# Second layer of a flow block: three buffers for split weights, 56 rows ahead with 14 parked, gathers over all rows, and a moved fold

## The chip, the cores and the metric

The kernel runs on one core of one Trainium2 chip. Its time is the device time of one execution, in microseconds (us). Five engines work beside each other, each on its own in-order queue: PE (matrix products; PEld is its loading of weights), DVE (vector work), ACT (scalar functions, copies, casts), POOL (here the indirect gathers) and SP (which issues most transfers). ACT and POOL issue some transfers too; 16 DMA engines carry all of them.

## The reference

Two layers, each with a mixer (gated unit, state-space scan, linear attention) and an expert part. The change touches the expert part of the second layer, for 256 tokens:

```python
def peer_ffn(h, w_query, sub_keys, expert_u, expert_v):    # blocks of 128 tokens
    q = (xb @ w_query).reshape(128, 8, 2, 128)
    s = einsum('thpd,phkd->thpk', q, keys)                 # 128 keys in each half
    s1, i1 = top_k(s[:, :, 0], 16);  s2, i2 = top_k(s[:, :, 1], 16)
    top_s, pos = top_k(s1[..., :, None] + s2[..., None, :], 16)
    idx = take_along_axis(i1 * 128 + i2, pos)              # 16 of 16384 experts, for each of 8 heads
    gate = softmax(top_s)
    act = gelu(einsum('td,thkd->thk', xb, expert_u[idx]))
    return einsum('thk,thkd->td', gate * act, expert_v[idx])
```

All is float32. Then follow a residual with a gate row and the last norm.

## The kernel before, in words

**Dense rows.** Instead of gathering 128 experts for each token, the kernel goes through all 16384 experts as 128 rows of 128 (NI1 = 128) and weighs what a token did not choose with zero. Row e has two halves. `U(e)` loads 128 vectors of expert_u (512 KB), splits them into a rounded part hi (ACT, L72) and a rest lo (DVE, L73), and PE multiplies both with the tokens (L1376, L1380) into the PSUM tile pu; ACT and DVE sum its two parts and apply GELU (L1398 to L1400). `V(e)` loads 128 vectors of expert_v, splits them the same way, multiplies the activations with the gates of row e (DVE, L1423), splits that product into whl (L1426 to L1429), and PE adds to four PSUM tiles acc (L1445). `stream` loads into `eraw` (five buffers) and has two buffers each for uhi, ulo, vhi and vlo.

**Gathered part.** In the second layer 192 of the 256 tokens go the dense way. For the other 64, `gather_rows` fetches the chosen experts' vectors by indirect DMA on POOL (L1300, 512 KB each): 64 u-items, which DVE multiplies and sums (L1306), and 64 v-items, which DVE adds into gacc (L1313). They share four `grow` buffers.

**Order.** `LEAD` rows of U are computed before the first V. They need only the tokens; the V rows need the gates, which `gates` makes at the same time: DVE writes one-hot matrices (108 operations, L1245 to L1253), PE multiplies them, ACT scales the result into a staging tile gst (two buffers of 16 KB a partition), and ACT's queue writes it to DRAM as gd (2 MB, six times, L1263). The gates of the first 8 rows stay on the chip; those of the others are read back as gt, four rows at a time (L1415). After the lead, V rows run alone until row LEAD - KEEP; from there each V row is paired with a U row. The first 8 activations of the lead stay in a buffer, the next `SPILL` rows are parked in DRAM (`aout` out, L1403; `ain` back, L1408), the rest stay on the chip.

`side()` is called once for each V row and once for each U row behind the lead. It adds `RATE` to an account, and takes the next gather items while the account is positive. The last three V rows go together (TOGETHER = 3). Then the 64 upper and 64 lower partitions of the last dense block are folded and joined to gacc by PE (L1514 to L1522), and the tail scales, adds, norms and stores.

A scheduler sets the final order of each engine's queue, so that the order in the program is a preference; a buffer's next writer waits for its last readers.

Of the kernel before, what the change touches and what calls it, by code (L numbers as in the profile page):

```python
# [10 lines left out]
F32 = mybir.dt.float32  # L11
F32R = mybir.dt.float32r
# [4 lines left out]
OP = mybir.AluOpType  # L17
# [11 lines left out]
PLAN = {"s5": ((4, 1, 0, 0, 0, 0), (4, 0, 0, 0, 0, 0)), "gla": ((1, 1, 1, 1, 0, 1, 1), (2, 2, 1, 1, 0, 1))}  # L29
DEPTH = 2  # L30
NI1 = 128
LEAD = {0: 40, 1: 64}
KEEP = 4
HOLD = {0: 4, 1: 8}
TOGETHER = {0: 4, 1: 3}
SPILL = {0: 22, 1: 32}
AHEAD = 2
ERAW = 5
GPS = 3
OHT = 8  # L40
OHB = 3
OSC = "av"
RATE = {0: 2.4, 1: 1.0}
NEG = -3.0e38


# [4 lines left out]
class Kernel:  # L51
# [1276 lines left out]
    def peer(self, l, dense):  # L1328
        nc, i = self.nc, self.i
        nb = len(dense)  # L1330
        half = self.half[l]
# [5 lines left out]
        with ExitStack() as es:  # L1337
            p = es.enter_context(self.pool(f"peer{l}"))
            acts_a = es.enter_context(self.pool(f"acta{l}"))
            es_b = es.enter_context(ExitStack())  # L1340
            acts_b = es_b.enter_context(self.pool(f"actb{l}"))
            lead, spill = LEAD[l], SPILL[l]
            per, away = 1024 // nt, {}
# [6 lines left out]
            p2 = es.enter_context(self.pool(f"peerv{l}", side="right"))  # L1350
            acc = [[pa.tile([128, 512], F32, name=f"acc{b}{h}", bufs=1) for h in range(2)] for b in range(nb)]
            acts, gt, rows, todo, left, los = {}, {}, {}, [], [], []

            def stream(src, nm):
                raw = p.tile([128, 1024], F32, name="eraw", bufs=ERAW)
                nc.sync.dma_start(raw, src)
                hi = p.tile([128, 1024], F32R, name=nm + "hi", bufs=2)
                lo = p.tile([128, 1024], F32R, name=nm + "lo", bufs=2)
                self.split(hi, lo, raw)
                return hi, lo  # L1360

# [48 lines left out]
            def V(e):  # L1410
# [6 lines left out]
                late = NI1 - 1 - e  # L1417
                hi, lo = stream(i["v"][l, e], "u" if late < TOGETHER[l] and late % 2 else "v")
# [14 lines left out]
                    return  # L1433

                for b in range(nb) if half is None else (1, 0):
                    for hs in ((0,), (1,)) if late == 0 else ((0, 1),):
                        for e_, hi, lo, w in todo:
                            if 128 * b + 128 > nt:

                                ops = [(w[:, 2 * nt - 64:], r) for r in (hi, lo)]  # L1440
                            else:
                                ops = [(w[:, o:o + 128], r) for o, r in ((128 * b, hi), (128 * b, lo), (nt + 128 * b, hi))]
                            for z, (a_, r) in enumerate(ops):
                                for h in hs:
                                    nc.tensor.matmul(acc[b][h], a_, r[:, 512 * h:512 * h + 512],  # L1445
                                                     start=e_ == 0 and z == 0, stop=e_ == NI1 - 1 and z == len(ops) - 1)
                todo.clear()

            def mod_load(l_, n, half):
                raws = []  # L1450
                for q in range(2):
                    raw = p.tile([128, 1024], F32, name="eraw", bufs=ERAW)
                    o = 2048 * half + 1024 * q
                    nc.sync.dma_start(raw, i["w_mod"][l_, n][:, o:o + 1024])
                    raws += [(raw, 0), (raw, 512)]
                return raws

            def pubank(shape, nm):
                t = pu_.tile([128, 512], F32, name="pu", bufs=8 - 2 * nb)
                n = math.prod(shape[1:])  # L1460
                return t[:, :n] if len(shape) == 2 else t[:, :n].rearrange("p (a b) -> p a b", b=shape[2])
            gb = self.gathered[l]
            gg = self.gather_gen(l, gb, es) if gb is not None or half is not None else iter(())
            mg = self.mod_gen(l, range(10, 12), mod_load, pubank, p, False)
            if not last:
# [15 lines left out]
            for e in range(NI1):  # L1481
# [5 lines left out]
                if e + KEEP == NI1:  # L1487
# [3 lines left out]
                    ep = es.enter_context(self.pool(f"peere{l}", side="right"))  # L1491
# [15 lines left out]
            out = {b: (acc[k][0], acc[k][1]) for k, b in enumerate(dense)}  # L1507
            if gb is not None:
                out[gb] = (self.gacc[:, 0:512], self.gacc[:, 512:1024])
            if half is not None:  # L1510

                out[half] = []
                fold = ep.tile([128, 64], F32, name="fold", bufs=1)
                nc.vector.tensor_tensor(fold, self.ident[:, 0:64], self.ident[:, 64:128], op=OP.add)  # L1514
                for h in range(2):
                    t = ep.tile([128, 512], F32, name="ft", bufs=2)
                    nc.scalar.copy(t, acc[nb - 1][h])
                    b = pubank([128, 512], "fold")
                    nc.tensor.matmul(b[0:64], fold, t, start=True, stop=True)
                    nc.tensor.matmul(b[64:128], fold, self.gacc[:, 512 * h:512 * h + 512], start=True, stop=True,  # L1520
                                     tile_position=(0, 64))
                    out[half].append(b)  # L1522
            for k, b in enumerate(sorted(out) if half is None else (3, 2)):
                ty = b // 2
                x = self.xk[b] = self.row([128, 1024], f"xe{b}")
# [2 lines left out]
                for h in range(2):  # L1528
                    hs = slice(512 * h, 512 * h + 512)
                    t = ep.tile([128, 512], F32, name="et", bufs=3)  # L1530
# [14 lines left out]
                else:  # L1545
# [6 lines left out]
                    for h, q in ((0, nc.sync), (1, nc.scalar)):  # L1552
                        hs = slice(512 * h, 512 * h + 512)
# [123 lines left out]
```

## Time and profile before

| | us |
|---|---|
| median of 3 runs (2687.3 to 2694.61) | 2690.12 |
| the profiled execution, its own time | 2692.46 |
| its span, first to last instruction | 2689.2 |
| PE busy (share of the span) | 2525.4 (94%) |
| DVE busy | 2185.1 (81%) |
| ACT busy | 1217.7 (45%) |
| POOL busy | 593.8 (22%) |

The program is a chain of stages, and busy time is a mean over all of them, so the shares in this table don't say what bounds a stage. A busy PE counts pipelined products whose ends are modelled. All that the change touches lies behind 1916 us, where the second layer's first U row is split on DVE.

### The profile page before, as it was taken

To read this page: it belongs to the slowest core of one execution; us is meant where nothing else is said; L and a number is where in the kernel's file an instruction comes from. 1 tells how busy PE (TensorE), PEld (TensorE's weight loads), DVE (VectorE), ACT (ScalarE), POOL (GpSimd) and SP (SyncE) were. 2 spreads that over 40 slices of the span, in tenths; PEclk is the share of its full clock that TensorE was granted. 3 is DMA by queue.
4 is the path that set the end of the run, shared out by engine and by line. 5 is a ranking of instruction groups with operands and counts; after the bars stand their busy time and mean duration, and the time that the engine had idled before them with its cause. 6 is when DMAs were issued, how large, how long until landed. Compare 5 with 4: busy or idle time off the path is not lost.

```text
span 2689.2 us, 42483 instructions
## 1 busy us (share of the span) xinstructions
PE 2525.4 (94%) x15591; PEld 2141.6 (80%) x15591; DVE 2185.1 (81%) x4639; ACT 1217.7 (45%) x2054; POOL 593.8 (22%) x468
## 2 busy tenths in 40 slices
PE   7999999999999999999999999999888977999997
PEld 4776888888778898998899996878877855677786
DVE  8765489999888988998988855837989788999985
ACT  3343343566434333333333333444457644555564
POOL 0001000010004433444443400010001043444500
PEclk8998999999999999999999999989899999999999
DMA  7521432587779899999999956625477899999984
GB/s 271 135 94 41 156 109 93 179 296 280 261 242 371 302 342 333 340 342 331 329 340 335 337 184 176 227 96 192 160 247 264 286 338 331 384 381 381 384 299 141
DMA packets 269200, 694.55 MB, mean 258 GB/s; under 512 B 28608, under 2 KB 120576, under 8 KB 266432
## 3 DMA queue, kind: packets, MB, share of 16 engines
q1 hardware_dynamic: 192960, 430.57, 47.3%
q0 software_dynamic: 55296, 201.35, 20.6%
q10 hardware_dynamic: 20736, 59.92, 6.3%
q8 instruction: 122, 2.00, 0.3%
q14 instruction: 86, 0.70, 0.1%
HBM read 631.84 MB, written 58.56 MB: 257 GB/s over the span
## 4 chain that ended last, share of the span: by engine, by line
PE 41%; issue 12%; DVE 10%; DMA 6%; ACT 4%; ACTq 0%; POOL 0%; SPq 0%; DVEq 0%; POOLq 0%
PE acc L1445 20%; PE pu L78 14%; PE pu L1376 2%; DMA act<-aout 2%; DVE ulo L73 2%; DVE vlo L73 2%; PE pu L1380 1%; ACT uhi L72 1%; DVE grow L1306 1%; DMA ain<-act 1%; ACT vhi L72 1%; PE prT L286 1%; DVE wlo L73 1%; DMA raw<-in_w_in_dram 1%; DVE gacc L1313 1%
## 5 line engine op out<-in xcount | busy, mean ns | idle before, releaser
L1445 PE MATMUL acc<-vhi,whl 128*128 128x512 f32 x2274 | 662.3, 401 | 27.1 <-ACT whl L1426 19.6
L1445 PEld LDWEIGHTS acc<-vhi,whl 128*128 128x128 f32 x2274 | 428.1, 190 | 131.3 <-ACT whl L1426 26.7
L72 ACT CAST vhi<-eraw 128x1024 fp32r<-128x1024 f32 x253 | 265.0, 1048 | 344.1 <-PE acc L1445 308.1
L1445 PE MATMUL acc<-vlo,whl 128*128 128x512 f32 x1264 | 395.4, 404 | 14.5 <-DVE vlo L73 14.0
L78 PE MATMUL pu<-hTb,uhi 128*128 128x384 f32 x2048 | 390.9, 341 | 7.7 <-ACT uhi L72 3.8
L73 DVE TENSOR_TENSOR vlo<-eraw,vhi 128x1024 fp32r<-128x1024 f32 x253 | 309.0, 1223 | 106.9 <-ACT vhi L72 106.3
L1300 POOL DMA_INDIRECT grow<-in_un_dram,gidx x192 | 243.9, 1270 | 603.3 <-DVE grow L1306 198.6
L78 PEld LDWEIGHTS pu<-hTb,uhi 128*128 128x128 f32 x2048 | 362.2, 190 | 17.3 <-ACT actr L1396 4.7
L73 DVE TENSOR_TENSOR ulo<-eraw,uhi 128x1024 fp32r<-128x1024 f32 x259 | 316.7, 1223 | 72.3 <-ACT uhi L72 57.9
L72 ACT CAST uhi<-eraw 128x1024 fp32r<-128x1024 f32 x259 | 272.0, 1051 | 183.5 <-PE pu L78 171.8
L1300 POOL DMA_INDIRECT grow<-in_v_dram,gidx x192 | 271.2, 1412 | 347.1 <-DVE gacc L1313 215.9
L1376 PE MATMUL pu<-hTb,uhi 128*128 128x384 f32 x1024 | 320.7, 369 | 18.0 <-ACT uhi L72 16.0
L1445 PEld LDWEIGHTS acc<-vlo,whl 128*128 128x128 f32 x1264 | 238.9, 191 | 82.8 <-DVE vlo L73 28.7
L1380 PE MATMUL pu<-hTb,ulo 128*128 128x192 f32 x1024 | 250.2, 265 | 25.7 <-DVE ulo L73 24.8
L1313 DVE SCALAR_TENSOR_TENSOR gacc<-grow,gact,gacc 128x1024 f32<-128x1024 f32 x190 | 243.9, 1284 | 1.8 <-DMA grow<-in_v_dram,gidx 1.7
L286 PE MATMUL prT<-hTb,whi 128*128 128x512 f32 (+1 forms) x928 | 240.2, 346 | 3.5 <-ACT whi L72 3.2
L1306 DVE SCALAR_TENSOR_TENSOR grow<-grow,h2n 128x1024 f32<-128x1024 f32 x192 | 234.4, 1221 | 8.8 <-DMA grow<-in_un_dram,gidx 8.8
L1380 PEld LDWEIGHTS pu<-hTb,ulo 128*128 128x128 f32 x1024 | 198.6, 196 | 48.5 <-DVE ulo L73 41.4
L1376 PEld LDWEIGHTS pu<-hTb,uhi 128*128 128x128 f32 x1024 | 195.1, 193 | 27.6 <-ACT uhi L72 22.6
L78 PE MATMUL pu<-hTb,ulo 128*128 128x384 f32 x1024 | 204.0, 337 | 0.5 <-DVE ulo L73 0.5
L73 DVE TENSOR_TENSOR wlo<-raw,whi 128x1024 fp32r<-128x1024 f32 x84 | 102.4, 1220 | 114.0 <-ACT whi L72 111.3
L286 PEld LDWEIGHTS prT<-hTb,whi 128*128 128x128 f32 x928 | 159.8, 190 | 31.3 <-ACT whi L72 3.4
(435 smaller groups left out, 3839.6 us busy)
## 6 DMA issues: line engine op xcount, KB each, us to landing
eraw<-in_ut_dram SPq DMA_DIRECT2D x256, 512.0 KB, 5.6
eraw<-in_v_dram SPq DMA_DIRECT2D x256, 512.0 KB, 6.0
gd<-gst ACTq DMA_DIRECT2D x18, 2048.0 KB, 8.2
mraw<-in_w_mod_dram SPq DMA_DIRECT2D x64, 512.0 KB, 5.1
gt<-gd SPq DMA_DIRECT2D x31, 768.0 KB, 10.2
raw<-in_w_in_dram SPq DMA_DIRECT2D x36, 512.0 KB, 5.3
raw<-in_w_query_dram SPq DMA_DIRECT2D x32, 512.0 KB, 3.9
eraw<-in_w_mod_dram SPq DMA_DIRECT2D x32, 512.0 KB, 6.3
```

What stands on the lines that cost most here:

```text
L72: (hi_eng or nc.scalar.copy)(hi, src)
L73: self.last_lo = (lo_eng or nc.vector).tensor_tensor(lo, src, hi.bitcast(F32), op=OP.subtract)
L78: self.nc.tensor.matmul(out, a, b, start=n == 0, stop=n == len(ops) - 1)
L286: self.nc.tensor.matmul(bs[g][:, pt * n:pt * n + n], a[:, k, gs], b, start=z == 0 and k == 0 and q == 0, stop=z == 1 and k == 3 and q == 2)
L1300: nc.gpsimd.indirect_dma_start(out=r, out_offset=None, in_=src, in_offset=bass.IndirectOffsetOnAxis(ap=idx[:, j:j + 1], axis=0))
L1306: v.scalar_tensor_tensor(r, r, 1.0, self.h2n, op0=OP.mult, op1=OP.mult, accum_out=act[:, j:j + 1])
L1313: v.scalar_tensor_tensor(acc, r, act[:, j:j + 1], acc, op0=OP.mult, op1=OP.add)
L1376: both = lambda: nc.tensor.matmul(pu, hi[:, cs], self.hTb[:, :, c, c0:c0 + nt], start=c == 0, stop=c == 7)
L1380: nc.tensor.matmul(pu[:, 0], lo[:, cs], hs(hh, c), start=False, stop=False)
L1445: nc.tensor.matmul(acc[b][h], a_, r[:, 512 * h:512 * h + 512], start=e_ == 0 and z == 0, stop=e_ == NI1 - 1 and z == len(ops) - 1)
```

## The change

In the second layer (in code: `half is not None`):
- `LEAD` falls from 64 to 56, so V rows run alone for 52 rows, not 60, and 72 U rows are paired, not 64. `SPILL` falls from 32 to 14.
- `RATE` falls from 1.0 to 0.72 gather items a call.
- `stream` has three buffers each for hi and lo of U and V. Those of V move from pool p to pool p2, which is opened when the gates are done.
- The folding of the last block moves from behind all rows to the last row's products, ahead of those for the second feature half of block 0; leftover gather items are taken before that.

```diff
-LEAD = {0: 40, 1: 64}
+LEAD = {0: 40, 1: 56}
-SPILL = {0: 22, 1: 32}
+SPILL = {0: 22, 1: 14}
-RATE = {0: 2.4, 1: 1.0}
+RATE = {0: 2.4, 1: 0.72}
...
-                hi = p.tile([128, 1024], F32R, name=nm + "hi", bufs=2)
-                lo = p.tile([128, 1024], F32R, name=nm + "lo", bufs=2)
+                q, n = (p, 2) if half is None else (p if nm == "u" else p2, 3)
+                hi = q.tile([128, 1024], F32R, name=nm + "hi", bufs=n)
+                lo = q.tile([128, 1024], F32R, name=nm + "lo", bufs=n)
...
                 for b in range(nb) if half is None else (1, 0):
+                    if late == 0 and b == nb - 1 and half is not None:
+                        for _ in gg:
+                            pass
                     for hs in ((0,), (1,)) if late == 0 else ((0, 1),):
+                        if late == 0 and half is not None and b == 0 and hs == (1,):
+                            folded()
...
+            def folded():
+                fold = ep.tile([128, 64], F32, name="fold", bufs=1)
+                nc.vector.tensor_tensor(fold, self.ident[:, 0:64], self.ident[:, 64:128], op=OP.add)
+                for h in range(2):
+                    t = ep.tile([128, 512], F32, name="ft", bufs=2)
+                    nc.scalar.copy(t, acc[nb - 1][h])
+                    b = pubank([128, 512], "fold")
+                    nc.tensor.matmul(b[0:64], fold, t, start=True, stop=True)
+                    nc.tensor.matmul(b[64:128], fold, self.gacc[:, 512 * h:512 * h + 512], start=True, stop=True,
+                                     tile_position=(0, 64))
+                    out2.append(b)
```

The same lines were behind the loops before. Layer one's instructions keep their order on every engine. In number only transfers change: 18 parked rows fewer go out on ACT's queue and come back on SP's.

**ACT at the end of the gates.** gst is the staging tile of gates, gd their place in DRAM; the brackets name the semaphores that an instruction waits for. Before:

```order
L1261 ACTIVATE gst<-gps 128x128x4 [waits PE_49]
L1263 DMA gd_18905<-gst 128x4096 [waits Activation_49]
L1398 COPY act<-pu 128x192 [waits PE_49]
L72 CAST uhi<-eraw 128x1024 [waits DMAHW4_49]
L1400 ACTIVATE act<-act 128x192 [waits DVE_49]
L1398 COPY act<-pu 128x192 [waits PE_49]
L72 CAST uhi<-eraw 128x1024 [waits DMAHW5_49]
L1400 ACTIVATE act<-act 128x192 [waits DVE_49]
```

After:

```order
L1261 ACTIVATE gst<-gps 128x128x4 [waits PE_49] x6
L1263 DMA gd_18905<-gst 128x4096 [waits DMAHW4_49,Activation_49]
L72 CAST vhi<-eraw 128x1024 [waits DMAHW4_49,Pool_49]
L1427 CAST whl<-act 128x192 [waits DVE_49]
L1430 CAST whl<-act 128x64
L72 CAST vhi<-eraw 128x1024 [waits DMAHW5_49]
```

Before, U rows follow the last write of gates. Now the first cast of V follows it at once. Its buffer lies where the second gst buffer lay, so it waits on DMAHW4_49, the semaphore that this write raises, as well as for POOL's copy of gst.

**DVE around the last gate operation** (oh1l, oh1h, oh, oh2s are the one-hot matrices; ulo the split of a U row). Before:

```order
L1399 TENSOR_TENSOR act<-act,pu 128x192
L1252 TENSOR_TENSOR oh1h<-oh1l,sel_19032 128x1024
L73 TENSOR_TENSOR ulo<-eraw,uhi 128x1024
L1253 TENSOR_TENSOR oh1l<-oh1l,sel_19032 128x1024
L1399 TENSOR_TENSOR act<-act,pu 128x192
L73 TENSOR_TENSOR ulo<-eraw,uhi 128x1024
L1399 TENSOR_TENSOR act<-act,pu 128x192
L73 TENSOR_TENSOR ulo<-eraw,uhi 128x1024
```

After:

```order
L73 TENSOR_TENSOR ulo<-eraw,uhi 128x1024
L1252 TENSOR_TENSOR oh1h<-oh1l,sel_18965 128x1024
L1253 TENSOR_TENSOR oh1l<-oh1l,sel_18965 128x1024
L1400 TENSOR_TENSOR act<-act,pu 128x192
L1253 TENSOR_TENSOR oh1l<-oh1l,sel_18965 128x1024
```

and, with no ulo between these two pieces:

```order
L1253 TENSOR_TENSOR oh1l<-oh1l,sel_19032 128x1024 x2
L1424 TENSOR_TENSOR act<-act,gt_19044 128x192 x2
L1460 TENSOR_TENSOR fold<-ident 128x64
L73 TENSOR_TENSOR vlo<-eraw,vhi 128x1024
L1428 TENSOR_TENSOR whl<-act,whl 128x192
```

Before, one gate operation stands behind the 51st U row and 13 U rows follow. Now the split of lead row 56, the last, stands ahead of 56 of the 108 gate operations, and the first V row follows the gates. Counted over the whole queue, 36 lead rows stand ahead of the first gate operation, 25 before. Gather items of DVE ahead of V row 53: 35; before, 54 ahead of V row 61. The last item stands near V row 116; before, near row 107.

**PE at the end** (pu<-ft,fold and pu<-gacc,fold are the fold). Before:

```order
L1445 MATMUL acc_19773<-vhi,whl 128x512
L1445 MATMUL acc_19773<-vlo,whl 128x512
L1445 MATMUL acc_19770<-vhi,whl 128x512
L1445 MATMUL acc_19771<-vhi,whl 128x512
L1519 MATMUL pu<-ft,fold 64x512
L1520 MATMUL pu<-gacc,fold 64x512
L1519 MATMUL pu<-ft,fold 64x512
L1520 MATMUL pu<-gacc,fold 64x512
```

After:

```order
L1451 MATMUL acc_19773<-vhi,whl 128x512
L1451 MATMUL acc_19773<-vlo,whl 128x512
L1451 MATMUL acc_19770<-vhi,whl 128x512
L1451 MATMUL acc_19771<-vlo,whl 128x512
L1451 MATMUL acc_19771<-vhi,whl 128x512
L1465 MATMUL pu<-ft,fold 64x512
L1466 MATMUL pu<-gacc,fold 64x512
L1465 MATMUL pu<-ft,fold 64x512
L1466 MATMUL pu<-gacc,fold 64x512
```

The fold still stands behind the last product of acc, with three of these products instead of two between it and the last of block 1.

## Rows read from the trace of the kernel before

**Rows 1.** The page, section 1: busy time of each engine, its share of the span, instructions.
```profile
PE 2525.4 (94%) x15591; PEld 2141.6 (80%) x15591; DVE 2185.1 (81%) x4639; ACT 1217.7 (45%) x2054; POOL 593.8 (22%) x468
```

**Rows 2.** Windows: busy us (instructions) of PE, PEld, DVE, ACT, POOL; PE clock, DMA share, GB/s.
```profile
2000.00:2106.00 106.00, 90.92 (x796) 83.36 (x795) 99.82 (x163) 74.78 (x138) 19.26 (x9) 0.97 0.77 268
2106.00:2138.00 32.00, 29.47 (x199) 27.13 (x196) 20.62 (x32) 20.44 (x43) 0.40 (x1) 1.00 0.87 304
2138.00:2165.00 27.00, 26.17 (x128) 21.84 (x129) 23.04 (x39) 15.93 (x34) 7.77 (x6) 1.00 0.83 271
2165.00:2284.00 119.00, 92.48 (x335) 64.34 (x333) 95.71 (x155) 49.36 (x101) 45.58 (x33) 0.94 0.96 341
2284.00:2343.00 59.00, 52.33 (x209) 38.89 (x208) 56.86 (x92) 30.13 (x64) 27.24 (x18) 0.97 1.03 388
2343.00:2553.00 210.00, 197.12 (x1053) 166.39 (x1052) 203.56 (x297) 121.81 (x245) 102.89 (x65) 1.00 1.00 381
2595.00:2640.00 45.00, 45.00 (x256) 40.72 (x256) 32.87 (x50) 28.66 (x59) 0.00 (x0) 1.00 0.84 256
```

**Rows 3.** DVE's timeline: start and length in us; four splits; last brackets: idle before.
```profile
2138.48 1.23 DVE L73 TENSOR_TENSOR vlo<-eraw,vhi 128x1024 fp32r<-128x1024 f32 x1 [1.78 <-ACT vhi L72]
...
2340.24 1.23 DVE L73 TENSOR_TENSOR ulo<-eraw,uhi 128x1024 fp32r<-128x1024 f32 x1
...
2650.09 1.22 DVE L73 TENSOR_TENSOR ulo<-eraw,uhi 128x1024 fp32r<-128x1024 f32 x1 [0.59 <-ACT uhi L72]
...
2654.70 1.23 DVE L73 TENSOR_TENSOR ulo<-eraw,uhi 128x1024 fp32r<-128x1024 f32 x1 [0.59 <-ACT uhi L72]
```

**Rows 4.** DVE's groups by form, 2000 to 2106: count, busy us, mean ns, idle before.
```profile
L73 DVE TENSOR_TENSOR ulo<-eraw,uhi 128x1024 fp32r<-128x1024 f32 x26 | 31.9, 1227 | 0.6 <-ACT uhi L72 0.5
L1251 DVE TENSOR_TENSOR oh1l<-iota,sel 128x1024 f16<-128x1024 f16 x24 | 16.8, 701 | 0.0
```

**Rows 5.** DVE's groups by form, 2343 to 2553.
```profile
L1313 DVE SCALAR_TENSOR_TENSOR gacc<-grow,gact,gacc 128x1024 f32<-128x1024 f32 x38 | 49.0, 1289 | 0.0
L73 DVE TENSOR_TENSOR vlo<-eraw,vhi 128x1024 fp32r<-128x1024 f32 x40 | 48.9, 1223 | 1.6 <-ACT vhi L72 1.2
...
L1306 DVE SCALAR_TENSOR_TENSOR grow<-grow,h2n 128x1024 f32<-128x1024 f32 x28 | 34.1, 1219 | 0.0
L1399 DVE TENSOR_TENSOR act<-act,pu 128x192 f32<-128x192 f32 x41 | 14.3, 349 | 0.7 <-ACT act L1398 0.7
...
L1306 DVE DVE_READ_ACCUMULATOR grow<-grow,h2n 128x1 f32 x28 | 2.3, 84 | 0.0
```

**Rows 6.** The chain of waits, 2040 to 2345: start, us, what.
```profile
2107.82 8.84 DMA gd<-gst
...
2131.73 5.65 DMA eraw<-in_v_dram
2137.41 1.05 ACT vhi L72
```

**Rows 7.** DMA issues, 2165 to 2284: KB each, median us to landing.
```profile
eraw<-in_v_dram SPq DMA_DIRECT2D x33, 512.0 KB, 6.3
gt<-gd SPq DMA_DIRECT2D x8, 384.0 KB, 7.2
ain<-act SPq DMA_DIRECT2D x28, 96.0 KB, 5.6
```

**Rows 8.** DVE's first group by form, 2165 to 2284.
```profile
L73 DVE TENSOR_TENSOR vlo<-eraw,vhi 128x1024 fp32r<-128x1024 f32 x33 | 40.2, 1223 | 16.3 <-ACT vhi L72 16.3
```

**Rows 9.** DVE's first group by form, 2284 to 2343.
```profile
L73 DVE TENSOR_TENSOR vlo<-eraw,vhi 128x1024 fp32r<-128x1024 f32 x21 | 25.5, 1223 | 2.1 <-ACT vhi L72 2.1
```

**Rows 10.** Waits, 2138 to 2343: us in total, times, longest.
```profile
ACT vhi L72 <- PE acc L1445: 38.7, 26, 3.2
```

**Rows 11.** The timeline of all engines at the end.
```profile
2673.68 0.64 PE L1519 MATMUL pu<-ft,fold 128*64 128x512 f32 x1
...
2674.81 0.69 DVE L1531 TENSOR_TENSOR et<-pu,gaterow 128x512 f32<-128x512 f32 x1 [5.47 <-PE pu L1520]
```

More of the change, by code (lines that the diff above doesn't have):

```diff
@@ L1447, in V, with mod_load @@
                 todo.clear()
-            def mod_load(l_, n, half):
+            out2 = []
+            def folded():
[9 more added lines that the diff above has]
+                    out2.append(b)
+            def mod_load(l_, n, part):
                 raws = []
@@ L1452, in mod_load @@
                     raw = p.tile([128, 1024], F32, name="eraw", bufs=ERAW)
-                    o = 2048 * half + 1024 * q
+                    o = 2048 * part + 1024 * q
                     nc.sync.dma_start(raw, i["w_mod"][l_, n][:, o:o + 1024])
@@ L1462, in peer @@
             gb = self.gathered[l]
+            ep = None
             gg = self.gather_gen(l, gb, es) if gb is not None or half is not None else iter(())
@@ L1510, in peer @@
             if half is not None:
[L1512 to L1522, printed above, removed]
+                out[half] = out2
             for k, b in enumerate(sorted(out) if half is None else (3, 2)):
```

## The prediction

> **What bounds the kernel now.** I read the page first, then the chain and DVE's timeline to find where the second layer's expert part begins and ends, then the windows of its stretches, then DVE's groups and the DMA issues inside a stretch, for prices. On the page PE looks like the bound [rows 1], but that mixes stages. The windows [rows 2] show what to look for: in each stretch another column is full. While one-hot gates and lead rows are made (2000 to 2106) DVE is busy 99.8 of 106 us. Then for 32 us lead rows fill PE (29.5 busy). From 2138 to 2343 only V rows run; with parked rows among them (2165 to 2284) DMA is 0.96 busy, yet at 341 GB/s, while PE and DVE both idle a fifth of the time; without (2284 to 2343) DMA moves 388 GB/s and DVE is busy 56.9 of 59. From 2343 to 2553 a U row is paired with each V row and gathers run too: DVE 203.6 of 210 and DMA 1.00. At last, when the gathers have run out, PE is busy 45.0 of 45. So DVE and DMA are overfull in one half and half empty in the other. The change moves work between these stretches; it removes little.
>
> Marks on DVE's timeline [rows 3]: the split of V row 0 starts at 2138.5, of U row 64 at 2340.2, of U row 127 at 2654.7. So the V-only stretch takes 201.8 us, the 63 steps of pairs 314.5, and the tail to 2689.2 follows.
>
> **Start of the V rows.** Eight lead rows fewer. In the order of DVE all 56 now stand ahead of the last gate operation, 50 before; these 6 more cost DVE (1.227 + 0.35) us each, less the overlap of neighbours. DVE's groups of 2000 to 2106, two of them shown, sum to 113 us where the window says 99.8, a factor of 0.88: 1.39 us a row, 8 us in all [rows 2, 4, 5]. The last write of gates, issued at 2107.8, so moves to 2116 if DVE stays as full. Before, its 8.84 us landing lay beside lead rows [rows 6]. Now it lies open: the new buffers of V stand where the gate staging tile stood, and the order shows ACT's first cast of V behind a wait for that write. Behind it on ACT's queue stand the casts of whl and all further V casts; DVE's first vlo and PE wait for those. 2116 + 8.84 + 1.05 (cast) gives 2126, 13 us earlier than 2138.5. But the last 56 of the 108 gate operations (0.70 us each, about 0.6 with overlap, 34 us [rows 4]) now run with no U row beside them, so what PE could not do ahead of them is lost; PE was busy 91 of 106 us in that stretch already, and 6 rows at half of a bare pair's 4.6 (below) are 14 us more. I take 8 us earlier; bounds 13 and 0. V's first load is no longer late (at 2131.7 it was issued behind the lead rows [rows 6]), which fills the wait with five loads ahead, no more.
>
> **V rows alone, 52 instead of 60** (with the two that DVE runs ahead, 54 for 62). A row's bytes [rows 7]: V 512 KB, a quarter of gt's 384 KB, a gather 512 KB, a parked row 96 KB. Gathers per row fall from about 0.9 to 0.66 (in the order: 35 by V row 53; before 54 by V row 61).
> - First 8: 23 us (27 in the window 2138 to 2165, less what its two late U rows took).
> - 14 parked rows: 512 + 96 + 96 + 0.66 x 512 = 1042 KB at that stretch's 341 GB/s is 3.13 us, 44 us. Before, 33 such rows took 119 us, 3.61 each [rows 2, 8].
> - 32 others: 946 KB at 388 GB/s is 2.50 us. DVE: in 2343 to 2553 the groups sum to 226 us for 203.6 busy, a factor of 0.90; a V row is (1.223 + 2 x 0.35) x 0.90 = 1.73 us and a gather (1.289 or 1.219 plus the 0.08 read) x 0.90 = 1.165, so 1.73 + 0.66 x 1.165 = 2.50 busy, 2.60 at the 96% of 2284 to 2343. Before, 21 rows took 59 us, 2.81 each [rows 2, 5, 9]. I take 2.65: 85 us.
>
> Sum 152 us against 201.8: 50 less. Bounds 145 (2.50 and 3.0 a row) and 158 (2.81, and 3.2 for the parked). ACT's waits for PE to release a vhi buffer (38.7 us, [rows 10]) are what the third buffer takes away; I give it nothing of its own, since behind them stands the next full column, DMA or DVE.
>
> **Pairs, 72 instead of 64.** Before, 40 pairs took 210 us, 5.25 each, with 65 gathers on POOL, 1.6 a pair [rows 2, 5]; then pairs without gathers at 4.6 (2650.1 to 2654.7, [rows 3]), where PE is full. Now gathers reach to V row 116, so 64 pairs carry (127 - 35) / 64 = 1.44 each and 8 none. DVE: ((2 x 1.223) + 3 x 0.35) x 0.90 = 3.15, plus 1.44 x 1.165 = 1.68: 4.83 busy, 4.98 at 97%. DMA: 1024 + 96 + 1.44 x 512 = 1857 KB at 381 GB/s is 4.99 us. Both give 5.0, PE's 4.6 lies below. 64 x 5.0 + 7 x 4.6 = 352 us against 314.5: 38 more. Bounds 4.83 (341 us) and the old 5.25 (368 us).
>
> **The edits at nothing.** The folded sums: on PE they still stand behind the last acc matmul, as the order shows; an earlier place could give back at most the 1.1 us from the first of them at 2673.7 to DVE's next operation at 2674.8 [rows 11]. They are not earlier: 0, bounds 0 and 1. The 18 parked rows fewer save writes under DVE-full time: 0 there; their reads are in the sum above.
>
> **Sum:** -8 - 50 + 38 = -20 us. The profiled execution took 2692.5, so 2672; it lies 2.3 above the runs' median of 2690.1, so 2670.
>
> **A rule against it.** In the stretch of pairs 381 GB/s were moved over 210 us, and 388 before that [rows 2]; I price by these. The Trainium skill, DMA: Bandwidth & Descriptors, section Bandwidth, says that for transfers between HBM and SBUF the HBM side binds at about 358 GB/s a core. By that rule a pair is 1.902 MB / 358 = 5.31 us and a plain V row 2.71: -8 - 48 + 57 = +1, no change at all. The trace disagrees with it by 6 to 8%, and the measurement decides. The first rival below is what it would be as a mechanism of this kernel.
>
> **Rivals.**
> - *DMA gives less when gathers run in every pair.* Place: the 64 pairs. For it: DMA shows 1.00 already, and where V rows, gathers and small reads mixed it moved only 341 GB/s [rows 2]. Against: that stretch had the parked rows' 96 KB reads, each 5.6 us to landing [rows 7]; pairs have none. At 341 a pair is 5.58 us, 64 x 5.58 + 32 = 389, V rows 158: -8 - 44 + 75 = +23, 2713. It decides from 5.45 us a pair on (349 GB/s): there the sum is +8. Slower.
> - *No start gain, no cheaper pair.* The gate tail plus the open write eat all of the earlier start, and a pair costs 5.2 with 1.44 gathers as with 1.6, because the in-order queues, not the amount, set it. 0 - 46 + 51 = +5 with 156 us of V rows; 2692 to 2697, no change. For it: in 2343 to 2553 three resources are near full at once, so none reaches its floor. Against: DVE waits only 3%.
> - *More than counted.* Three buffers let DVE reach its busy time alone: pairs 4.83, V rows 2.5, start 13 earlier: -13 - 57 + 27 = -43, 2647. For it: the 38.7 us of ACT waits and a PE that idles a fifth. Against: DMA would have to move 394 GB/s.
>
> **Chances.** About 0.3% (8 us) is what a measurement of this kernel can tell from no change. Forecast (8 to 33 us less): 0.62. More than counted: 0.15. No gain: 0.12. DMA gives less: 0.11, of which 0.07 is slower by over 8 us and 0.04 is near the even point. Faster 0.77, same 0.16, slower 0.07. The range goes from 2650, the near edge of the third rival, to 2692, where the no-gain case lies: 2 in 10 stay out. The forecast's own range is 2657 to 2682.
>
> **What would show it.** V row 0's vlo at about 2130 behind an ACT gap of some 9 us ended by the gate write; U row 56 at about 2282; then 64 pairs of 5.0 us with DVE near 97% and DMA near 1.0, and only 8 bare ones at 4.6; U row 127 at about 2634; the tail as before. Wrong if the gates end after 2125, if pairs cost over 5.2, or if PE waits longer for V's split parts though they have three buffers.

## The result, and the profile after

The changed kernel takes 2654.97 us (median of 4 runs, 2653.18 to 2658.18), the kernel before 2688.85 (4 runs, 2687.3 to 2694.61): a ratio of 0.9878, 95% interval 0.9856 to 0.9899. The forecast was 2670, in a range of 2650 to 2692: the direction and the range held, and the gain was 34 us where 20 were forecast. The time lies 2 us below the forecast's own, narrower range of 2657 to 2682. The profiled execution took 2654.35 us, its span 2652.5.

The page of the changed kernel, section 1 (busy time, share, instructions), answers to [rows 1]:

```profile
PE 2508.3 (95%) x15591; PEld 2142.3 (81%) x15591; DVE 2179.1 (82%) x4639; ACT 1218.6 (46%) x2054; POOL 620.1 (23%) x468
```

The shares hardly moved, as a shift of work between stages would have it. Its windows, with the columns of [rows 2], cut at the new boundaries of the stages:

```profile
2020.00:2070.00 50.00, 49.26 (x416) 46.65 (x414) 50.00 (x81) 39.25 (x73) 3.84 (x5) 1.00 0.78 269
2070.00:2113.00 43.00, 32.16 (x310) 29.00 (x310) 42.44 (x73) 29.32 (x53) 11.98 (x4) 0.82 0.65 258
2113.00:2125.00 12.00, 3.34 (x30) 2.98 (x28) 1.98 (x6) 3.73 (x7) 0.40 (x1) 0.50 0.45 189
2125.00:2143.00 18.00, 18.00 (x72) 14.51 (x73) 17.38 (x30) 11.48 (x26) 5.87 (x3) 0.90 0.95 329
2143.00:2193.00 50.00, 42.11 (x161) 31.31 (x160) 41.92 (x75) 23.74 (x48) 17.73 (x12) 0.93 0.99 350
2193.00:2268.00 75.00, 71.29 (x298) 54.28 (x297) 73.10 (x122) 42.38 (x90) 48.27 (x21) 1.00 1.03 385
2268.00:2588.00 320.00, 306.31 (x1651) 260.87 (x1650) 307.05 (x448) 189.52 (x383) 145.83 (x88) 1.00 1.00 376
2588.00:2614.00 26.00, 26.00 (x149) 23.58 (x148) 22.88 (x34) 20.23 (x38) 0.00 (x0) 1.00 0.92 319
```

Read from the top: lead rows and gates, where PE and DVE are both full; gates (2070 to 2113; the last four lead rows are split in the first 10 us of it, then gates run alone), where DVE is full and PE idles a quarter; a hole of 12 us in which nothing is full; eight V rows; V rows with parked activations; plain V rows; 64 pairs with gathers; bare pairs. The hole is new. Between its edges stands what [rows 6] held before, now on ACT's timeline (start, length, instruction, idle before it and what ended it):

```profile
2117.31 0.33 ACTq L1263 DMA_DIRECT2D gd<-gst  x1
2123.66 1.04 ACT L72 CAST vhi<-eraw 128x1024 fp32r<-128x1024 f32 x1 [6.37 <-DMA gd<-gst]
```

and DVE's timeline with the marks of [rows 3], the splits of V row 0, U row 56, U row 120 (the first pair without gathers) and U row 127, with the last two gate operations, joined in one line, ahead of them:

```profile
2112.67 1.28 DVE L1253 TENSOR_TENSOR oh1l<-oh1l,sel 128x1024 f16<-128x1024 f16 x2
...
2124.73 1.23 DVE L73 TENSOR_TENSOR vlo<-eraw,vhi 128x1024 fp32r<-128x1024 f32 x1 [6.19 <-ACT vhi L72]
...
2268.36 1.23 DVE L73 TENSOR_TENSOR ulo<-eraw,uhi 128x1024 fp32r<-128x1024 f32 x1 [0.74 <-ACT uhi L72]
...
2589.97 1.23 DVE L73 TENSOR_TENSOR ulo<-eraw,uhi 128x1024 fp32r<-128x1024 f32 x1 [0.17 <-ACT uhi L72]
...
2614.07 1.23 DVE L73 TENSOR_TENSOR ulo<-eraw,uhi 128x1024 fp32r<-128x1024 f32 x1 [0.35 <-ACT uhi L72]
```

Against the marks of [rows 3]: V row 0 starts 13.75 us earlier; the V-only stretch takes 143.6 us, not 201.8 (58.2 less); the pairs 345.7, not 314.5 (31.2 more); and from U row 127 to the end of the span 38.4, not 34.5 (3.9 more). -13.75 - 58.2 + 31.2 + 3.9 = -36.85, and the spans differ by 36.7: all of the gain is in these four pieces. The two profiled executions lie 38.1 apart, the medians 33.9; where each profile lies among its runs accounts for the rest.

DVE's first groups by form in 2143 to 2193 and 2193 to 2268, which answer to [rows 8] and [rows 9]:

```profile
L73 DVE TENSOR_TENSOR vlo<-eraw,vhi 128x1024 fp32r<-128x1024 f32 x16 | 19.6, 1224 | 4.6 <-ACT vhi L72 4.6
...
L73 DVE TENSOR_TENSOR vlo<-eraw,vhi 128x1024 fp32r<-128x1024 f32 x29 | 35.3, 1219 | 0.5 <-ACT vhi L72 0.5
```

DVE's groups in 2268 to 2588 (without the split by form), which answer to [rows 5]:

```profile
L73 DVE TENSOR_TENSOR ulo<-eraw,uhi 128x1024 fp32r<-128x1024 f32 x64 | 78.2, 1223 | 12.8 <-ACT uhi L72 12.8
L73 DVE TENSOR_TENSOR vlo<-eraw,vhi 128x1024 fp32r<-128x1024 f32 x63 | 76.8, 1219 | 0.0
L1313 DVE SCALAR_TENSOR_TENSOR gacc<-grow,gact,gacc 128x1024 f32<-128x1024 f32 x54 | 69.3, 1282 | 0.0
L1306 DVE SCALAR_TENSOR_TENSOR grow<-grow,h2n 128x1024 f32<-128x1024 f32 x38 | 46.3, 1218 | 0.0
```

That is 64 pairs, with 92 gather items (54 and 38), 1.44 a pair; from U row 56 to U row 120 they take 321.6 us, 5.03 each. ACT's waits, 2125 to 2268 (us in total, times, longest), answer to [rows 10]:

```profile
ACT vhi L72 <- PE acc L1451: 8.4, 8, 1.3
```

### The profile page after: what moved, and what is told of

The parts are those of the page before. It is cut to its first block, busy times and chain, and to the rows that moved or that the text cites. A ratio compares the mean times of both kernels' runs of the same rounds, so it can differ in the third digit from the quotient of the medians.

```text
span 2652.5 us, 42384 instructions
## 1 busy us (share of the span) xinstructions
PE 2508.3 (95%) x15591; PEld 2142.3 (81%) x15591; DVE 2179.1 (82%) x4639; ACT 1218.6 (46%) x2054; POOL 620.1 (23%) x468
## 4 chain that ended last, share of the span: by engine, by line
PE 59%; DVE 21%; issue 8%; DMA 8%; ACT 4%; POOL 0%; SPq 0%; ACTq 0%; DVEq 0%; POOLq 0%
PE pu L78 20%; PE acc L1451 19%; PE prT L286 4%; PE prN L300 2%; PE pu L1377 2%; DVE vlo L73 2%; DVE ulo L73 2%; DVE gacc L1313 2%; PE opp L953 1%; ACT uhi L72 1%; DVE grow L1306 1%; DVE wlo L73 1%; PE modp L158 1%; PE pu L1381 1%; PE gps L1259 1%
## 5 line engine op out<-in xcount | busy, mean ns | idle before, releaser
L1451 PE MATMUL acc<-vhi,whl 128*128 128x512 f32 x2274 | 652.8, 397 | 16.9 <-ACT whl L1427 15.4
L1451 PEld LDWEIGHTS acc<-vhi,whl 128*128 128x128 f32 x2274 | 426.9, 189 | 111.4 <-ACT whl L1427 17.7
L1451 PE MATMUL acc<-vlo,whl 128*128 128x512 f32 x1264 | 390.1, 400 | 11.8 <-DVE vlo L73 11.6
L1300 POOL DMA_INDIRECT grow<-in_un_dram,gidx x192 | 253.2, 1319 | 572.2 <-DVE grow L1306 181.7
L78 PEld LDWEIGHTS pu<-hTb,uhi 128*128 128x128 f32 x2048 | 364.4, 191 | 17.4 <-ACT actr L1397 4.7
L1300 POOL DMA_INDIRECT grow<-in_v_dram,gidx x192 | 288.5, 1502 | 368.6 <-DVE gacc L1313 208.7
L1306 DVE SCALAR_TENSOR_TENSOR grow<-grow,h2n 128x1024 f32<-128x1024 f32 x192 | 234.0, 1220 | 10.8 <-DMA grow<-in_un_dram,gidx 10.8
```

The source lines that it names most:

```text
L78: self.nc.tensor.matmul(out, a, b, start=n == 0, stop=n == len(ops) - 1)
L1300: nc.gpsimd.indirect_dma_start(out=r, out_offset=None, in_=src, in_offset=bass.IndirectOffsetOnAxis(ap=idx[:, j:j + 1], axis=0))
L1306: v.scalar_tensor_tensor(r, r, 1.0, self.h2n, op0=OP.mult, op1=OP.mult, accum_out=act[:, j:j + 1])
```

## The experiments

The theory: the gain is a shift of gathers from the V-only rows and of U rows from the lead into stretches that had room, and the third buffers and the fold carry none of it. The rival: the third buffers free ACT's casts and so DVE and DMA. The table has the marks of all kernels on DVE's timeline beside the times (V0 behind the last gate operation, both by their starts; V-only, from V0 to the first paired U row; pairs, to U row 127; medians, and ratios to the runs of the kernel before that were taken beside them). In the changed kernel, e1, e5, e6 and e11 the timeline joins the last two gate operations in one line, and the column counts from the first of them, 0.64 us earlier.

| | V0 at | behind gates | V-only | pairs | median us | ratio (95%) |
|---|---|---|---|---|---|---|
| before | 2138.5 | 36.4 | 201.8 | 314.5 | 2688.85 | 1 |
| after | 2124.7 | 12.1 | 143.6 | 345.7 | 2654.97 | 0.9878 (0.9856 to 0.9899) |
| e1 three buffers alone | 2144.9 | 11.6 | 194.3 | 306.5 | 2684.43 | 0.9994 (0.9981 to 1.0006) |
| e2 spread alone | 2139.4 | 35.6 | 178.9 | 315.7 | 2668.24 | 0.9931 (0.9919 to 0.9944) |
| e3 lead 56, 24 parked | 2121.1 | 17.3 | 169.9 | 352.6 | 2679.98 | 0.9975 (0.9964 to 0.9986) |
| e4 after, two buffers | 2113.6 | 16.7 | 146.5 | 350.8 | 2649.01 | 0.9865 (0.9850 to 0.9880) |
| e5 after, fold as before | 2128.5 | 10.8 | 144.8 | 345.6 | 2652.65 | 0.9863 (0.9836 to 0.9891) |
| e6 after, gst shifted | 2125.7 | 10.9 | 144.5 | 345.9 | 2652.04 | 0.9862 (0.9834 to 0.9889) |
| e9 after, U two, V three | 2116.1 | 16.7 | 148.0 | 349.9 | 2649.86 | 0.9858 (0.9831 to 0.9885) |
| e10 e9, 1 parked | 2112.3 | 16.0 | 137.4 | 352.6 | 2640.53 | 0.9827 (0.9799 to 0.9854) |
| e11 e6, fold constant early | 2112.2 | 6.1 | 148.3 | 346.3 | 2651.24 | 0.9873 (0.9854 to 0.9893) |
| e12 e10, rate 0.66 | 2111.1 | 16.6 | 134.5 | 361.8 | 2638.42 | 0.9827 (0.9807 to 0.9848) |
| e13 e10, V two | 2119.5 | 16.1 | 138.4 | 349.7 | 2637.47 | 0.9820 (0.9800 to 0.9840) |
| e14 e10, lead 50, 0 parked | 2106.5 | 12.1 | 119.7 | 381.6 | 2643.84 | 0.9850 (0.9829 to 0.9871) |

The second layer's first U row starts anywhere from 1912.7 to 1921.1 in these profiles, so lengths compare better than places.

### Each part alone: e1, e2, e3

e1, the buffers, against the kernel before:

```diff
-                hi = p.tile([128, 1024], F32R, name=nm + "hi", bufs=2)
-                lo = p.tile([128, 1024], F32R, name=nm + "lo", bufs=2)
+                q, n = (p, 2) if half is None else (p if nm == "u" else p2, 3)
+                hi = q.tile([128, 1024], F32R, name=nm + "hi", bufs=n)
+                lo = q.tile([128, 1024], F32R, name=nm + "lo", bufs=n)
```

> The kernel before with nothing but the third buffers (V's in the later pool): 64 rows ahead, 32 parked, gathers at 1.0. Theory A (the gain is the even spread of work over rows; buffers alone give little, since behind the released wait stands DMA in the V rows and DVE in the pairs): 2680 to 2694 us, pairs with gathers still 5.2 us, parked V rows still 3.4 to 3.6 us. Theory B (the third buffers give most of it, by letting U rows run ahead under the gates and by taking away ACT's 38.7 us of waits for a vhi buffer): 2670 us or less, the first V split at least 10 us earlier than 2138.5, V rows under 3.1 us.

Measured: 0.9994, 2684.43 us, inside theory A's range. Its windows (columns as above):

```profile
2133.00:2145.00 12.00, 3.40 (x43) 3.10 (x42) 2.80 (x9) 4.51 (x11) 0.40 (x1) 0.75 0.64 265
2145.00:2339.00 194.00, 160.00 (x609) 116.83 (x610) 168.09 (x277) 90.80 (x189) 87.46 (x53) 0.95 0.98 348
2339.00:2550.00 211.00, 196.00 (x1063) 167.51 (x1062) 205.97 (x301) 125.19 (x247) 98.94 (x66) 1.00 1.02 388
```

The hole of 12 us is here too, at 64 lead rows: it comes with the buffers, not with the shorter lead. With a third buffer all U rows of the lead slip ahead of the gates' end, none is left to lie beside the last gate write, and V row 0 starts 6.4 us later than before. The V-only stretch and the pairs take 7.4 and 8.0 us less, and the end behind U row 127 is 4.3 longer (probably U runs further ahead of the V rows with a buffer more, so that part of this is the mark that moves and not the work). In sum -4.7 in the profiles, and nothing that the runs can tell.

e2, the spread, against the kernel before:

```diff
-RATE = {0: 2.4, 1: 1.0}
+RATE = {0: 2.4, 1: 0.72}
```

> The kernel before with nothing but RATE 0.72 in place of 1.0. Theory A: 14 gathers leave the V-only rows (18 us less there) for bare pairs (13 us more): 2680 to 2686 us. Theory B: no change, 2686 to 2692, because two buffers and the parked rows keep the V rows at their pace.

Measured: 0.9931, 2668.24 us, some 19 us less: the largest part, by one number, and more than theory A expected (2680 to 2686). Windows:

```profile
2139.00:2318.00 179.00, 157.56 (x646) 117.51 (x647) 155.70 (x257) 92.73 (x192) 71.97 (x42) 0.99 0.97 342
2318.00:2634.00 316.00, 303.69 (x1622) 258.55 (x1622) 299.54 (x437) 187.65 (x379) 130.29 (x83) 0.99 1.00 372
```

V0 stays where it was, the V-only rows lose 22.9 us with 14 gather items fewer among them (42, where before had 56), and the pairs cost 1.2 more (18 and 13 were expected). 22.9 / 14 = 1.6 us an item where a gather's DVE work is 1.165 (the prediction's price) and its 512 KB at 342 GB/s are 1.53: there a gather cost about what its bytes do. Among the pairs it was nearly free: DVE's last gather item stands 13 us ahead of U row 127, before 82, so bare pairs were filled.

e3, the lead, against the kernel before (24 parked, so that as many rows wait on the chip as before):

```diff
-LEAD = {0: 40, 1: 64}
+LEAD = {0: 40, 1: 56}
...
-SPILL = {0: 22, 1: 32}
+SPILL = {0: 22, 1: 24}
```

> The kernel before with LEAD 56 and SPILL 24 (as many activations stay on the chip as before, 8 fewer rows parked), two buffers, RATE 1.0. Theory A: the stretch in which lead rows fill PE alone is 14 us shorter, 8 V rows alone fewer save 25, 8 pairs more cost 42, 8 parked rows fewer give back 5: 2684 to 2692 us. Theory B: the same, the lead alone is worth nothing.

Measured: 0.9975, 2679.98 us, some 4 us below theory A's range. V0 17.4 us earlier, V-only 31.9 less, pairs 38.1 more. The spread, the lead and the buffers alone give -0.69, -0.25 and -0.06%, 1.0% in all; the change gives 1.22, and the ten parked rows that e3 kept are worth, by the price that e10 shows, an estimated 7 us or 0.27% more.

### The change with one part undone: e4, e5, e9

e4, two buffers each, V's still in pool p2:

```diff
-                q, n = (p, 2) if half is None else (p if nm == "u" else p2, 3)
+                q, n = (p, 2) if half is None else (p if nm == "u" else p2, 2)
```

> The changed kernel with two split buffers instead of three, all else as changed (V's still in the later pool, 56 ahead, 14 parked, 0.72). Theory A: 2656 to 2664 us; pairs with gathers 5.0 to 5.1 us. Theory B: 2672 us or more; first V split later than 2130, pairs 5.2.

Measured: 2649.01, ratio 0.9865, 7 us below theory A's range and far from theory B's. Windows:

```profile
2050.00:2097.00 47.00, 42.12 (x378) 37.96 (x379) 47.00 (x78) 35.27 (x66) 1.20 (x3) 1.00 0.74 266
2097.00:2113.00 16.00, 15.66 (x121) 14.69 (x118) 11.40 (x20) 12.60 (x28) 0.40 (x1) 1.00 0.83 307
2113.00:2260.00 147.00, 133.57 (x561) 100.69 (x560) 133.71 (x226) 79.70 (x166) 70.07 (x36) 1.00 1.01 367
2260.00:2580.00 320.00, 306.04 (x1645) 259.92 (x1644) 306.42 (x448) 189.28 (x383) 143.74 (x88) 1.00 1.00 376
```

With two buffers six lead rows stay behind the last gate operation, and they lie beside the gate write: the hole is gone (PE 15.66 of 16). Counted from the second layer's first U row, the gates end 12 us earlier than in the changed kernel and V0 comes 7 us earlier. The pairs run as with three: 376 GB/s, DVE 306.4 of 320. So the third buffers carry none of the gain. Whether they cost something isn't settled: the medians lie 6 us apart, but each was taken beside other runs of the kernel before, and the intervals of the ratios overlap.

e5, the fold back behind all rows:

```diff
-                    if late == 0 and b == nb - 1 and half is not None:
-                        for _ in gg:
-                            pass
...
-                        if late == 0 and half is not None and b == 0 and hs == (1,):
-                            folded()
...
-                out[half] = out2
+                out[half] = []
+                fold = ep.tile([128, 64], F32, name="fold", bufs=1)
...
```

> The changed kernel with the fold back behind all rows (and no early end of the gathers). Theory: the fold's matmuls stand last on PE in both, so 0: 2653 to 2657 us and the same tail. Rival: the moved fold costs or gives 2 to 4 us at the tail, whose length from the split of U row 127 is 38.4 us after the change and 34.5 before.

Measured: 0.9863, 2652.65 us; from U row 127 to DVE's last operation 32.2 us, as in the changed kernel. The fold's new place gives nothing. PE's timeline of the changed kernel shows why, as the order did: the fold is still last on PE, behind the last product of acc.

```profile
2636.66 0.39 PE L1451 MATMUL acc<-vhi,whl 128*128 128x512 f32 x1
2636.98 0.64 PE L1465 MATMUL pu<-ft,fold 128*64 128x512 f32 x1
...
2638.32 0.59 PE L1466 MATMUL pu<-gacc,fold 128*64 128x512 f32 x1
```

e9 keeps the third buffer for V alone:

```diff
-                q, n = (p, 2) if half is None else (p if nm == "u" else p2, 3)
+                q, n = (p, 2) if half is None else ((p, 2) if nm == "u" else (p2, 3))
```

> The changed kernel with two buffers for U's split and three for V's. Theory C (three U buffers let the lead run out ahead of the gates, so the last gate operations and the last write have nothing beside them: 11 us later start; three V buffers give 3 us in the V rows and 5 in the pairs): first V split near 2114 as with two of both, V rows 144, pairs 346 to 349: 2642 to 2646 us. Rival (the loss is V's place or its third buffer): 2652 to 2657 us, start near 2125.

Measured: 0.9858, 2649.86 us, the same as e4's and above the range of theory C, whose start came (V0 at 2116.1) and whose gain from V's third buffer did not (V-only 148.0, not 144; pairs 349.9). V0 comes 16.7 us behind the last gate operation, as in e4, with lead rows between. So at this lead it is U's third buffer that opens the hole. But e5 and e6, which have it, ran on the same chip at 0.9863 and 0.9862: the hole as a whole costs nothing that these runs can tell.

### The hole itself: e6, e11

e6 takes one more gst tile ahead of the gates, so that the last write leaves from the other buffer, not from the place where the first vhi lies:

```diff
         with self.pool(f"gate{l}", side="right") as p:
+            if l == 1:
+                nc.vector.memset(p.tile([128, NI1, 32], F32, name="gst", bufs=2)[:, 0:1, 0:1], 0.0)
```

> The changed kernel with one gate staging tile allocated ahead of the six (a memset of one column), so that the last of them lies in the other buffer and V's first cast waits for the fifth write of gates, issued 9.5 us earlier, not for the sixth. Theory C (the open write costs the start of the V rows): the first V split 6 us earlier than 2124.7, and 2648 to 2651 us. Rival: the time comes back as a wait for the read-back of gates or for DMA in the V rows: 2653 to 2657 us.

Measured: 0.9862, 2652.04 us, between the two ranges; V0 at 2125.7 was not earlier. ACT no longer waits for the write, and DVE does, in front of the fold constant, which the scheduler had put ahead of the first vlo (both timelines):

```profile
2119.56 1.04 ACT L72 CAST vhi<-eraw 128x1024 fp32r<-128x1024 f32 x1 [0.45 <-POOL gt L1264]
...
2125.52 0.22 DVE L1462 TENSOR_TENSOR fold<-ident 128x64 f32<-128x64 f32 x1 [5.29 <-DMA gd<-gst]
2125.66 1.22 DVE L73 TENSOR_TENSOR vlo<-eraw,vhi 128x1024 fp32r<-128x1024 f32 x1
```

A tile that is used in the last microseconds of the kernel waits here for gst's write, and its one short operation, early on an in-order queue, held the first V row as long as the cast had. The write was waited for twice; taking away one wait showed the other. e11 takes away both, by making the constant ahead of the gates:

```diff
+            if half is not None:
+                fold = p.tile([128, 64], F32, name="fold", bufs=1)
+                nc.vector.tensor_tensor(fold, self.ident[:, 0:64], self.ident[:, 64:128], op=OP.add)
...
-                fold = ep.tile([128, 64], F32, name="fold", bufs=1)
-                nc.vector.tensor_tensor(fold, self.ident[:, 0:64], self.ident[:, 64:128], op=OP.add)
```

> As the run with the shifted gate staging tile, and the constant of the fold is made ahead of the gates, since in that run DVE's fold operation, ahead of the first V split in its queue, took over the wait for the last write of gates (5.3 us). Theory C: now nothing of the V rows' start waits for that write; the first V split comes 5 us earlier, measured from the last gate operation (6 us behind it, not 11 to 12), and the time is 3 to 5 us below the changed kernel's: 2648 to 2652 us. Rival: the rows that come earlier meet DMA, which has the same bytes to move: V-only rows get longer by as much, 2652 to 2656 us.

Measured: 0.9873, 2651.24 us. That lies in theory C's range, but the V-only rows got longer, as the rival had it (148.3 us, 144.5 in e6). On DVE's timeline the hole is half as long, and there is a new one, at V row 5:

```profile
2106.11 1.28 DVE L1255 TENSOR_TENSOR oh1l<-oh1l,sel 128x1024 f16<-128x1024 f16 x2
...
2112.18 1.23 DVE L73 TENSOR_TENSOR vlo<-eraw,vhi 128x1024 fp32r<-128x1024 f32 x1 [0.41 <-ACT vhi L72]
...
2128.13 1.23 DVE L73 TENSOR_TENSOR vlo<-eraw,vhi 128x1024 fp32r<-128x1024 f32 x1 [4.22 <-ACT vhi L72]
```

SP's timeline of the same run says what that cast had waited for. The last write of gates was issued at 2110.68; SP's queue stands at the read-back of gates until it has landed, and the loads of V stand behind it:

```profile
2117.09 0.97 SPq L1421 DMA_DIRECT2D gt<-gd  x2
...
2118.99 10.72 SPq L1361 DMA_DIRECT2D eraw<-in_v_dram  x6
```

In the changed kernel SP's queue reads the same, 8.7 us behind the issue of the write instead of 8.3:

```profile
2123.71 0.96 SPq L1416 DMA_DIRECT2D gt<-gd  x2
...
2125.98 19.01 SPq L1356 DMA_DIRECT2D eraw<-in_v_dram  x9
```

So the write had a third waiter. V row 0 comes 6.1 us behind the last gate operation, not 12.1, the five rows whose loads lie ready run, and the next one stands for its load. The first eight rows take 23.4 us where the changed kernel's take 18.7, and V row 8 is 29.5 us behind the last gate operation, not 30.8: of 6 us 1.3 are left, and the runs don't show them.

### Further: e10, e12, e13, e14

e10 parks 1 row instead of 14, e9 otherwise; the room is that of U's third buffer:

```diff
-SPILL = {0: 22, 1: 14}
+SPILL = {0: 22, 1: 1}
```

> As the run with two U and three V buffers, with the space of U's third buffer given to activations: 1 parked row instead of 14. By the price found for parked rows (3.1 us against 2.6 for a plain V row, 13 rows) 6 us less than that run: 2636 to 2640 us. Rival: nothing, because DMA or DVE is full there anyway.

Measured: 2640.53 (0.9827) against e9's 2649.86 on the same chip, with no run of either among those of the other: 9.3 us, 0.7 a row, where 6 were expected. Nearly all of it lies in V rows 8 to 24, of which e9 parks 14: 52.3 us there, 41.1 in e10. Windows of these rows, of e9 and of e10:

```profile
2137.00:2189.00 52.00, 42.10 (x164) 30.48 (x163) 41.38 (x72) 24.14 (x49) 17.02 (x12) 0.97 0.94 329
```

```profile
2130.00:2171.00 41.00, 39.65 (x169) 30.82 (x168) 41.00 (x75) 24.48 (x50) 23.13 (x12) 1.00 1.03 386
```

Thirteen reads of 96 KB are 1.28 MB, 3.9 us at 329 GB/s, and the stretch is 11 us shorter: the other 7 are a higher rate, 386 GB/s. DVE is busy as long in both (41.4 and 41.0 us); what goes is its idle time. With the parked rows neither DVE (41.4 of 52) nor DMA (0.94) is full: before the gate product DVE waits 4.1 us in all for parked rows to land, and before vlo 5.2, most of it for ACT's casts. How much of the lower rate comes from small reads as such, and how much from rows that stand in order behind them, these runs don't separate.

e12 to e14 are e10 with a lower rate of gathers, with two buffers for V, and with a lead of 50 and no parked row.

```diff
-RATE = {0: 2.4, 1: 0.72}
+RATE = {0: 2.4, 1: 0.66}
```

> As the run with two U buffers, three V buffers and 1 parked row (2640.5 us), with RATE 0.66 in place of 0.72, so that the gathers last until the bare pairs are nearly gone. Theory A (even spread): 7 bare pairs at 4.6 are filled, each gather pair gets 0.1 gathers less (0.12 us on 64 pairs) and V rows 3 gathers less: 2632 to 2637 us. Rival: pairs with fewer gathers stay at 5.0 us, since DMA and DVE are both full, so that the 7 pairs more cost 3 us: 2641 to 2645 us.

```diff
-                q, n = (p, 2) if half is None else ((p, 2) if nm == "u" else (p2, 3))
+                q, n = (p, 2) if half is None else (p if nm == "u" else p2, 2)
```

> As the run with two U buffers, three V buffers and 1 parked row (2640.5 us), with two V buffers too. Theory: V's third buffer is worth nothing (the runs with two and three of them at 14 parked rows differ by 1 us): 2638 to 2643 us. Rival: 4 us or more slower, since without parked rows V rows run at DVE's pace and every wait counts.

```diff
-LEAD = {0: 40, 1: 56}
+LEAD = {0: 40, 1: 50}
...
-SPILL = {0: 22, 1: 1}
+SPILL = {0: 22, 1: 0}
```

> As the run with two U buffers, three V buffers and 1 parked row (2640.5 us), with 50 rows ahead and none parked. Theory: the 6 lead rows behind the last gate operation covered the last write of gates; without them the first V split comes only 4 to 6 us earlier instead of 14, 6 V rows alone fewer save 15, 6 pairs more cost 30: 2646 to 2653 us, so that 56 is about as far as the lead can fall. Rival: the lead may fall further: 2636 us or less.

Measured: 0.9827, 0.9820 and 0.9850 (2638.42, 2637.47 and 2643.84 us), beside e10's 0.9827. e12 lies between its two ranges, e13 half a us below its theory's, and e14 some 2 us below its theory's. At 0.66 the V-only stretch lost 2.9 us and the pairs took 9.2 more, while the end from U row 127 to DVE's last operation fell from 28.1 to 22.8: no gain, and of the two rates neither is better. Two buffers for V are as good as three, as far as the intervals tell. A lead of 50 makes V rows and pairs about as dense as in e10, in windows of its run:

```profile
2106.00:2226.00 120.00, 114.42 (x467) 88.18 (x468) 116.76 (x201) 70.43 (x147) 66.11 (x32) 0.97 1.01 372
2226.00:2546.00 320.00, 304.73 (x1639) 258.89 (x1639) 305.20 (x449) 187.71 (x382) 145.00 (x90) 1.00 1.00 377
```

The hole opens here with two U buffers too, since no lead row is left behind the gates; ACT's first cast of V waits again:

```profile
2105.40 1.04 ACT L72 CAST vhi<-eraw 128x1024 fp32r<-128x1024 f32 x1 [6.38 <-DMA gd<-gst]
```

So what covers the write is lead rows behind the last gate operation, and a third U buffer is one way to lose them. V0 comes 5.9 us earlier than in e10 and the V-only stretch is 17.7 shorter; six more pairs cost 29.0. -5.9 - 17.7 + 29.0 = +5.4, and the profiles' spans differ by 5.4 (2642.1 and 2636.7). Work only changes places there, between stretches that are equally full.

e10, e12 and e13 are the fastest, 1.7 to 1.8% below the kernel before, and below the changed kernel by some 0.5%.

## Why the prediction was right, and which terms were mis-sized

The sum -8 - 50 + 38 became -13.75 - 58.2 + 31.2, and 3.9 at the end for which nothing had been counted. Each of the three forecast terms missed in the same direction, two of them (start and V-only rows) beyond their bounds, and the tail took back a little: the mechanism was right, and the total missed the forecast's own range.

**Where the gain lies.** Right, as a step: V-only rows less by more than the pairs take back, with DMA or DVE full on both sides. e2 and e3 show the two halves of it apart.

**Pairs, 5.0 us each.** Measured 321.6 us for 64, 5.03 each, with DVE busy 307 of 320 and DMA 1.00: as forecast, to the count of gathers in them (1.44). The first rival, that DMA gives less when gathers run in every pair, fell: 376 GB/s were moved over these 320 us, and it needed 349 or less. The second rival, no cheaper pair, fell too. The rule that the prediction set against itself stands in the Trainium skill, DMA: Bandwidth & Descriptors, section Bandwidth: for transfers between HBM and SBUF the HBM side binds at about 358 GB/s. The trace does not agree, with 376 GB/s over 320 us and 385 over the 75 before. The same section of the Trainium skill, DMA: Bandwidth & Descriptors, gives about 358 GB/s as what each core gets when both cores of an HBM domain stream. The prediction left that condition out; this kernel ran on one core.

**The bare pairs and the end.** 7 x 4.6 us and 34.5 behind them were forecast, 66.7 in all; measured 24.1 (U row 120 to 127) and 38.4, 62.5. The tail, forecast "as before", is 3.9 longer and the bare pairs are 8.1 shorter. U row 127 comes earlier against the rest, and what follows it is longer. That goes with U's third buffer: from U row 120 to DVE's last operation it is 56.3 us, and in e4 with two buffers 57.0, but there U row 127 comes 28.2 us behind U row 120, not 24.1.

**The V-only stretch, 152.** Measured 143.6, 1.4 below the bound of 145. The parked rows came out in size (V row 8 to 24, 14 of these 16 parked, in 49.7 us, 3.11 a row, 3.13 forecast). Their price was bytes at a rate read from rows with the same small reads, so that DVE's waits for them, which e9 shows, were in it without being named. The plain rows came nearly (2.60, 2.65 forecast). Mis-sized were the first eight (18.7 us, not 23: the price came from a window of before in which two late U rows had been taken off by estimate), and the count (53 rows up to U row 56, not 54 and the step to it).

**The start, 8 us earlier.** Mis-sized: 13.75, just over the upper bound of 13, and 17.1 when measured from the second layer's first U row (1916.0 before, 1919.3 after). The chain that gave 13 came out: the last write of gates was issued at 2117.31 (2116 forecast), ACT's cast behind it waited as named ([6.37 <-DMA gd<-gst]), the write landed in 6.26 us where 8.84 had been counted, and V row 0 started at 2124.73 where this sum gave 2126. What failed is the step behind it. Five of the 13 us were taken off for PE work that gates alone would leave undone; the trace shows no such delay, since DVE was busy 42.4 and PE only 32 of the 43 us in which the gates end. A count was off as well: on DVE's timeline of the kernel before, 49 lead rows stand ahead of the last gate operation, not 50 or 51; 13 lie between it and V row 0, and two behind that. In the changed kernel 53 gate operations, not 56, follow the last lead row.

Removing a lead row can save more than DVE's price of 1.39 us. Before, 13 U rows ran behind the gates in the 36.4 us from the last gate operation to V row 0, 2.8 each, and with two buffers e3 and e4 show 2.4 and 3.0 for each of the 8 rows (V0 19.3 and 24.3 us earlier from the first U row; e4 also parks ten rows fewer than e3). Of that the changed kernel gives some back, for the hole.

**The third buffers, nothing of their own.** Right. ACT's waits for PE to release vhi fell from 38.7 us [rows 10] to 8.4 (32.9 in e4's V-only stretch, with two buffers), and e1, e4 and e13 show that they bought no time. The Trainium skill, Perfetto Trace Analysis, section Optimization Strategy, says that a gap that repeats on the engine that should be saturated can mean that there are too few buffers. Here the gap was on ACT, which is not that engine (30 busy of 59 us in the best V-only window of [rows 2]), and the runs show that filling it gained nothing (e1, 0.9994).

**The fold, nothing.** Right, by e5.

**Against the third rival** ("more than counted", 2647): the measured time lies between it and the forecast, nearer to it in size and not in its reason. The start came 13.75 earlier, as it had it, but the pairs are at 5.03 and not at 4.83, and the buffers did not do it.

What stays open: what, if anything, the third buffers cost in the changed kernel. e4, e9, e5 and e6 lie within 4 us of each other, which their intervals don't separate. Why rows with 96 KB reads among the loads run at a lower rate was not tried either, nor what it would bring to take away all three waits for the last write.

## What to carry to other kernels

Balance stages by their full columns: when one stretch is full in DMA and DVE and another has steps with room in both (here pairs without gathers), spreading the optional work evenly, here by one number, can be worth more than buffers for an engine that waits on the side. Price a removed step by the pace of the place where it stood, not by the engine that is full elsewhere. When a deeper buffer lets work run ahead, look for what it had covered: a wait that is opened so may sit on several in-order queues at once (here ACT's, DVE's and SP's). Taking away two of the three brought nothing here that the runs show; that the last would pay was not tried.

## What the runs showed of the hardware that was not expected

The granted clock follows the hole. In the changed kernel's windows it is 0.82 of full speed while gates end (PE busy 32 of 43 us), 0.50 in the 12 us of the hole (the lower level, 1.2 of 2.4 GHz), 0.90 and 0.93 in the next 68 us, and 1.00 from 2193 on. In e4, whose lead rows cover the same place, it is 1.00 in all four windows shown (PE 15.66 of 16 in that place).

A DMA share near 1 is not one rate. In the changed kernel V rows with parked ones among them showed 0.99 and moved 350 GB/s (2143 to 2193), plain ones 1.03 and 385 (2193 to 2268).
